# Aligned overflow joins, zero products around the expert stages, a later first map, all next keys in the layer change, and a shared final scaling

## The chip, the cores and the metric

One core of one Trainium2 chip. The time is that of the device in microseconds, from the first to the last work of one launch; less is better. All arithmetic is in float32, with products of two-part (high and low) operands where accuracy needs it.

## The reference

Two transformer blocks of two layers each, on 256 tokens of width 1024, one after the other. Cut to what matters here:

```
for l in range(2):                        # first block
    x = layer_norm(alpha * x + mixer(x), ...)            # gated linear attention and spatial gating
    x = layer_norm(alpha * x + mem_xattn(x, mem), ...)   # k = mem @ wk[l], v = mem @ wv[l]
    x = layer_norm(alpha * x + grouped_moe(x), ...)      # 16 experts, top 2 of one group of 4
for l in range(2):                        # second block
    x = x + gate_m * mixer(rmsnorm(x) * (1 + scale_m) + shift_m)
    x = x + gate_f * grouped_moe_2(rmsnorm(x) * (1 + scale_f) + shift_f)
out = rmsnorm(x, final_norm)
# an expert: y += gate[:, e] * ((silu(x @ w_gate[e]) * (x @ w_up[e])) @ w_down[e])
```

## The kernel before

Everything is one program of straight code on the five engines, with a scheduler that orders the instructions of each engine by priority (the order of the source, and `tc.high_priority` ahead of it) and a simulated time line, except where an order is fixed: inside the expert loop PE runs in the order of the source (`tc.manual_schedule`), and in `start()` PE, DVE and ACT do. `tc.issue_after(ins)` puts what it encloses behind an instruction. Weights come through one DMA queue (SP) into rings of buffers.

There are four expert stages (`moe`): layers 0 and 1 of the first block (stages 1 and 2), layers 0 and 1 of the second (stages 3 and 4). A stage begins with `start()`: the choice of two experts for every token on DVE, five small position products (`pos`), then `gather` products that collect the tokens of experts 0 to 3 into 64 slots each (`xg`), a quarter of the features at a time, with an affine map out of PSUM on ACT or DVE. For features 512 and up the gathers need the second half of the low part `yzl`, written by `low(1)`. The gate weights of the map are written to `turner`. Then, expert by expert:

- `turned` and `down` of the expert before (`ht`, `dn`), `slot_map` (`one` on DVE, `pt` on PE, `pmap` and `wcol` on DVE), the gate and up products of this expert (`front`, tile `gu`, 32 products each), with `down` of the expert before behind the second of the eight steps of the gate product, and for expert 0 `rest()` behind the fourth: the gathers of features 512 and up;
- an overflow test, `tc.If(counts[e] > 64)` (L949): for the rare expert with over 64 tokens a long body follows that works through the rest (`overflows`, with its own tests at L818 and L820). All others jump past it. Each engine has its own copy of the branch. `foretell` puts a hint of the coming branch into PE's code;
- `scatter` of the expert before into four accumulators `y` (L773), and for the next four experts two gathers at a time.

After the last expert `finish_now` scales its result (`ds`) and scatters it (L768). `busy(ins, n)` issues n products of a zero matrix of 128x512 into an accumulator; the kernel before uses it in the overflow bodies alone, and `awake` is a similar helper at the end of stage 2.

Between stage 1 and the next layer ("the layer change") the first half of the memory keys of layer 1 is made (`mem_k(l + 1, kT, 0, memT)`), each weight row split into a high part on ACT (L165) and a low part on DVE (L166); the second half is made in `mem_kv` of layer 1, behind the first mixer. The layer norm between them (`residual_ln`) has priority, and `token_major` (L480, L487, L488) is the row-wise scaling that is put off. `ada` products and sums (L1231, L1236) prepare the modulation of the second block all along.

At the end `rms_tokens` squares y on ACT, a chain of small DVE operations (`rsqrt`, L304 to L313) gives the scale, and four DVE operations (L1789) write z, each followed by its store on SP (L1790).

Of the kernel before, what the change touches and what calls it, by code (L numbers as in the profile page):

```python
# [10 lines left out]
FT = mybir.dt.float32  # L11
# [4 lines left out]
OP = mybir.AluOpType  # L16
# [4 lines left out]
D = 1024  # L21
# [53 lines left out]
def kernel(ctx: ExitStack, tc: tile.TileContext, a: dict, out: bass.AP):  # L75
# [105 lines left out]
    def affine(dst, src, scale, bias, eng=None):  # L181
        e = eng
        if e is None:
            turn[0] += 1
            e = "S" if turn[0] % 2 else "V"
        if e == "S":
            S.activation(dst, src, AF.Identity, bias=bias, scale=scale)  # L187
        else:
            V.tensor_scalar(dst, src, scale, bias, op0=OP.mult, op1=OP.add)
# [444 lines left out]
    def moe(second, lg, rows, rs, nb, c, g, b, names, l, between):  # L634
# [41 lines left out]
        def gather(sel, xg, w, f0, bank):  # L676

            per = 512 // w
            ps = bank("xg", (128, per, w))
            for j in range(per):  # L680
                fs = slice((f0 + j) * 128, (f0 + j + 1) * 128)
                for i, z in enumerate((zh, zh, zl, zl)):
                    PE.matmul(ps[:, j, :], z[:, i % 2, fs], sel[:, i % 2, :], start=i == 0, stop=i == 3)  # L683
            turn[0] += 1
            for j in range(per):
                f = f0 + j
                affine(xg[:, f, :], ps[:, j, :], g[:, f:f + 1], b[:, f:f + 1], "SV"[turn[0] % 2])

        def front(hs, xs, ws, bank, w=64, early=lambda ins: None, half_way=lambda: None):

# [162 lines left out]
        def start():  # L853

            for tt in range(2):
                V.scalar_tensor_tensor(p[:, tt, :], lg[:, tt, :], rs[:, tt:tt + 1], c[:, 0, :], op0=OP.mult, op1=OP.add)
            normal(0, 0)
            if second:
                S.activation(w, p, AF.Exp, scale=-1.0)
            else:  # L860
                mx = tiny("mx", [128, 2])
                V.tensor_reduce(mx, p, axis=AX.X, op=OP.max)
                V.tensor_tensor(w, p, mx[:, :, None].to_broadcast([128, 2, E]), op=OP.subtract)
                S.activation(w, w, AF.Exp)
            high(0, 0)
            for q, tt in ((0, 1), (1, 0), (1, 1)):
                normal(q, tt)
                high(q, tt)
            if second:
                with tc.issue_after(last[1]):  # L870
                    residual(0, 3 - l)
                V.tensor_scalar(w, w, 1.0, None, op0=OP.add)
                V.reciprocal(w, w)
                V.tensor_tensor(p, w, rb[:, 1:2, :].to_broadcast([128, 2, E]), op=OP.add)
                mb = select_top2(p, p)
            else:
                for tt, c_ in ((0, 1), (1, 0), (1, 1), (0, 0)):
                    PE.matmul(y[tt][c_], zerob, zerob[:, None, :].to_broadcast([128, 4, 128]), start=True, stop=False,
                              skip_group_check=True)
                mb = select_top2(p, w)  # L880
            pp = wk("pos", (128, 3, E))
            PE.matmul(pp[:, 0, :], before, mb[:, 0, :], start=True, stop=True)
            PE.matmul(pp[:, 1, :], onesb, mb[:, 0, :], start=True, stop=False)
            PE.matmul(pp[:, 1, :], before, mb[:, 1, :], start=False, stop=True)
            PE.matmul(pp[:, 2, :], onesb, mb[:, 0, :], start=True, stop=False)
            PE.matmul(pp[:, 2, :], onesb, mb[:, 1, :], start=False, stop=True)
            if second:
                residual(3 - l, 4)
            low(0)
            V.scalar_tensor_tensor(posm, pp[:, 0:2, :], 1.0, mb, op0=OP.add, op1=OP.mult)  # L890
            sel = choose(0, 4, posm)
            V.tensor_copy(cnt, pp[0:1, 2, :])
            xg = slots_of(0)
            turn[0] = 0
            gather(sel, xg, 256, 0, wk)
            gate = gates(mb, w)
            rest_ = tiny("grest", [128, 2, E])
            V.tensor_copy(gparts[:, :, :, 0], gate)
            V.tensor_tensor(rest_, gate, gparts[:, :, :, 0], op=OP.subtract)
            V.tensor_copy(gparts[:, :, :, 1], rest_)  # L900
            V.tensor_tensor(gparts[:, :, :, 2], rest_, gparts[:, :, :, 1], op=OP.subtract)
            low(1)
            gather(sel, xg, 256, 2, wk)
            return sel, xg

        for tt in range(2):
# [2 lines left out]
            sel, xg = start()  # L909

        def rest():
            nonlocal gh
            for f0 in (4, 6):
                gather(sel, xg, 256, f0, wk)
            if not second:
                gh = between()
# [6 lines left out]
            with tc.issue_after(ins):  # L923
                tc.mark_branch_hint_location(f"over{second}{l}{e}", engines=[mybir.EngineType.PE])

        gh, late, pend = None, [], None
        more(len(ring) + 1 - FIRST)
        with tc.manual_schedule(engines={mybir.EngineType.PE}):
            for e in range(E):
                i = e % 4  # L930
                ws = weights[e]
                hs, hp = t1("hs", [128, 256]), t1("hp", [128, 2, 128])
                counts[e] = nc.values_load(cnt[0:1, e:e + 1], min_val=0, max_val=T)
                if pend:
                    hs_, hp_, wd = pend
                    turned(hp_, hs_, wk)
                maps_, maps = (maps, mapped(e)) if e else (None, mapped(e))
                xs = xg[:, :, i * 64:(i + 1) * 64]

                def early(ins):  # L940
                    if e < 2:
                        foretell(e, ins)
                    if pend:
                        finish(down(hp_, wd, wk), maps_[1], ds)
                        more(2)

                front(hs, xs, ws, wk, early=early, half_way=(lambda: None) if e else rest)
                more(4 - (e == ONCE // 6))
                with tc.If(counts[e] > 64, label=f"over{second}{l}{e}"):  # L949
                    overflows(e, ws)  # L950
                if pend:
                    ins = scatter(maps_[0], ds)
                    if e + 1 < E:
                        foretell(e + 1, ins)
                if i == 2 and e + 2 < E:
                    nsel = choose(e + 2, 4, posm)
                    nxg = slots_of(e // 4 + 1)
                    for f0 in range(0, NK, 2):
                        late.append(lambda f0=f0, s_=nsel, x_=nxg: gather(s_, x_, 256, f0, wk))
                for _ in range(2):  # L960
                    if late:
                        late.pop(0)()
                if e == 0:
                    if second:
                        gh = between()
                    else:
                        residual()
                pend = hs, hp, ws[2]
                if i == 3 and e + 1 < E:
                    sel, xg = nsel, nxg  # L970
            turned(hp, hs, wk)
            finish_now(down(hp, ws[2], wk), maps[1], maps[0], ds)
        return y


# [158 lines left out]
    def mem_kv(l, kT=None):  # L1134

        memT = memory()
        first = kT is None
        if first:
            kT = keys()
        vm = b8("vm", (128, 2, D))  # L1140
        V.memset(vm[:, 0, 0:1], 0.0)
        if l == 0:
            more = tables()
            next(more)
        if first:
            mem_k(l, kT, 0, memT)
        mem_k(l, kT, 1, memT)
        if l == 0:
            list(more)
        fill("c", l)  # L1150
        for q in range(2):
            for tt, p in enumerate(proj(cut("wv_x", l, cuts=CUT512, i=q), 0, 512, memT, "vmp")):
                cp(vm[:, tt, q * 512:(q + 1) * 512], p)
        return kT, vm
# [585 lines left out]
    for l in range(DEPTH):  # L1740
# [8 lines left out]
                lambda: token_major(rows, rows_of(l, 1, "xtok"), place=rows, wait=True))  # L1749
        if l + 1 < DEPTH:  # L1750
            memT, kT = memory("xl"), keys()
            mem_k(l + 1, kT, 0, memT)
            residual_ln(y, l, 2)
        else:
            rs = last_ln(y, l)
    for l in range(DEPTH):
# [23 lines left out]
        else:  # L1780
            fB = act.tile([128, D], FT, name="fB", tag="b4", bufs=4)
            src = a["final_row"]
            SP.dma_start(fB, bass.AP(tensor=src.tensor, offset=src.offset, ap=[[0, 128], [1, D]]))
    rs = rms_tokens(y)
    for tt in range(2):
        z = act.tile([128, D], FT, name="z", tag="z", bufs=4)
        for q in range(2):
            s = slice(q * 512, (q + 1) * 512)
            V.scalar_tensor_tensor(z[:, s], y[tt][q], rs[:, tt:tt + 1], fB[:, s], op0=OP.mult, op1=OP.mult)  # L1789
            SP.dma_start(out[0, tt * 128:(tt + 1) * 128, s], z[:, s])  # L1790


def _lay(w, cuts):
# [142 lines left out]
```

## Time and profile before

| | |
|---|---|
| median of 3 runs | 1836.7 us (1836.13 to 1842.41) |
| profiled execution | 1834.16 us, span 1832.4 us |
| mean granted clock of TensorE | 0.967 |
| PE busy | 1677.5 us (92%) |
| DVE, ACT busy | 882.6 us, 597.6 us |
| DMA | 570.44 MB, mean 311 GB/s; about 411 GB/s in the expert stages |

PE is TensorE's matrix unit, PEld its weight loads, PEq (or PEldq) its sequencer. "A <- B" in a view of waits says that A on its engine sat idle until B was done; "issue" means that the profile shows nothing that it waited for. Times inside the span are counted from its start. [...]

### The profile page before, as it was taken

How to read it: one execution, taken by the hardware profiler on the slowest of the kernel's cores; microseconds unless marked ns; L12 is line 12 of the kernel's file. 1: busy time of each engine (PE TensorE's matmuls, PEld its weight loads, DVE VectorE, ACT ScalarE, POOL GpSimd, SP SyncE). 2: the span in 40 equal slices, each digit the busy share in tenths (PEclk: the TensorE clock that was granted, in tenths of full speed). 3: DMA queues.
4: the chain of work that ended last, by engine and by line, in shares of the span. 5: the costliest groups of instructions: out<-in, count | busy, mean ns of one | idle time of the engine just before them, and what ended most of it. 6: DMA issues, size and time to landing. Idle time of an engine off the chain costs nothing. (4 is left out here: it accounts for less than half of the span.)

```text
span 1832.4 us, 31259 instructions
## 1 busy us (share of the span) xinstructions
PE 1677.5 (92%) x12127; PEld 1178.6 (64%) x12127; DVE 882.6 (48%) x2328; ACT 597.6 (33%) x1277; POOL 1.6 (0%) x10
## 2 busy tenths in 40 slices
PE   8999989998897998999989998898989899898987
PEld 7799855555686996555548776555545777554553
DVE  7887542222589966222247686322222546432322
ACT  5555322112364554111124554211111444221111
POOL 0000000000000000000000000000000000000000
PEclk9999989999898999999999999999999988999998
DMA  9758779999675786899997455899964872799793
GB/s 371 277 188 343 275 303 391 412 411 403 277 283 182 276 329 225 355 412 411 410 402 308 176 189 199 321 384 413 413 270 154 357 290 99 293 413 412 288 413 126
DMA packets 105790, 570.44 MB, mean 311 GB/s; under 512 B 11725, under 2 KB 14575, under 8 KB 56088
## 3 DMA queue, kind: packets, MB, share of 16 engines
q1 hardware_dynamic: 105064, 566.15, 78.5%
q8 instruction: 181, 2.97, 0.7%
q14 instruction: 113, 0.93, 0.1%
q10 hardware_dynamic: 432, 0.40, 0.1%
HBM read 565.44 MB, written 3.16 MB: 310 GB/s over the span
## 5 line engine op out<-in xcount | busy, mean ns | idle before, releaser
L696 PE MATMUL gu<-w,xg 128*64 128x256 f32 x4096 | 476.1, 384 | 11.9 <-ACT xg L187 8.3
L696 PEld LDWEIGHTS gu<-w,xg 128*64 128x64 f32 x4096 | 297.1, 138 | 184.1 <-issue 40.2
L165 ACT ACTIVATE wp<-w 128x512 fp32r<-128x512 f32 (+5 forms) x416 | 224.8, 548 | 220.7 <-PE pj L494 77.5
L166 DVE TENSOR_TENSOR wp<-w,wp 128x512 fp32r<-128x512 f32 (+5 forms) x416 | 235.8, 584 | 92.0 <-ACT wp L165 90.2
L724 PE MATMUL dn<-w,hp 128*64 128x512 f32 x1024 | 242.0, 609 | 9.5 <-issue 8.1
L724 PEld LDWEIGHTS dn<-w,hp 128*64 128x64 f32 x1024 | 79.4, 141 | 133.8 <-issue 113.8
L494 PE MATMUL pj<-xh,wp 128*128 128x256 f32 x800 | 155.8, 292 | 6.0 <-DVE wp L166 4.8
L494 PEld LDWEIGHTS pj<-xh,wp 128*128 128x128 f32 x800 | 129.3, 196 | 9.7 <-DVE wp L166 5.3
L756 DVE SCALAR_TENSOR_TENSOR ds<-dn,wcol,ds 64x512 fp32r<-64x512 f32 x60 | 45.0, 750 | 179.9 <-ACT ds L755 167.9
L703 DVE TENSOR_TENSOR hs<-hs,gu 128x256 f32<-128x256 f32 x64 | 26.9, 421 | 204.3 <-ACT hs L702 203.2
L494 PE MATMUL pj<-xl,wp 128*128 128x256 f32 x400 | 114.5, 288 | 0.3 <-DVE xl L166 0.3
L702 ACT ACTIVATE hs<-gu 128x256 f32<-128x256 f32 x64 | 24.5, 384 | 231.5 <-PE gu L696 231.0
L755 ACT ACTIVATE ds<-f,onesf 64x512 fp32r<-64x512 f32 x60 | 43.2, 720 | 170.0 <-DVE f L747 169.3
L773 PE MATMUL y<-ds,pmap 128*128 128x512 f32 x240 | 70.8, 417 | 27.6 <-PEq L949 25.5
L755 ACT ACTIVATE ds<-dn,wcol 64x512 fp32r<-64x512 f32 x60 | 40.9, 682 | 169.2 <-PE dn L724 144.8
L747 DVE SCALAR_TENSOR_TENSOR f<-dn,wcol,gh 128x512 f32<-128x512 f32 x32 | 24.0, 751 | 147.2 <-PE dn L724 138.2
L494 PEld LDWEIGHTS pj<-xl,wp 128*128 128x128 f32 x400 | 78.4, 196 | 1.1 <-DVE xl L166 0.5
L773 PEld LDWEIGHTS y<-ds,pmap 128*128 128x128 f32 x240 | 40.9, 190 | 58.4 <-issue 41.3
L1236 DVE SCALAR_TENSOR_TENSOR as<-w,cs,as 128x512 f32<-128x512 f32 x91 | 67.9, 746 | 0.5
L683 PE MATMUL xg<-sel,yzh 128*128 128x256 f32 x256 | 54.0, 291 | 8.9 <-issue 5.1
L756 DVE SCALAR_TENSOR_TENSOR ds<-f,onesf,ds 64x512 fp32r<-64x512 f32 x60 | 44.9, 748 | 22.4 <-ACT ds L755 21.4
L683 PE MATMUL xg<-sel,yzl 128*128 128x256 f32 x256 | 52.6, 288 | 0.0
(546 smaller groups left out, 2493.4 us busy)
## 6 DMA issues: line engine op xcount, KB each, us to landing
w<-in_moe_w_gate_dram SPq DMA_DIRECT2D x54, 1024.0 KB, 10.7
w<-in_ada_w_dram SPq DMA_DIRECT2D x48, 1024.0 KB, 6.9
w<-in_w_down_dram SPq DMA_DIRECT2D x44, 1024.0 KB, 15.0
w<-in_moe_w_up_dram SPq DMA_DIRECT2D x44, 1024.0 KB, 12.6
w<-in_w_up_dram SPq DMA_DIRECT2D x40, 1024.0 KB, 12.0
w<-in_w_gate_dram SPq DMA_DIRECT2D x38, 1024.0 KB, 12.2
w<-in_moe_w_down_dram SPq DMA_DIRECT2D x34, 1024.0 KB, 12.5
w<-in_moe_w_down_dram SPq DMA_DIRECT2D x60, 512.0 KB, 12.6
```

Of the source, the lines that this page charges most:

```text
L165: ins = S.activation(hi, src, AF.Copy)
L166: eng.tensor_tensor(lo, src, hi.bitcast(FT), op=OP.subtract)
L494: ins = PE.matmul(out, lhs[x], rhs[y], start=first and i == 0, stop=last and i == 2, **kw)
L683: PE.matmul(ps[:, j, :], z[:, i % 2, fs], sel[:, i % 2, :], start=i == 0, stop=i == 3)
L696: end = PE.matmul(gu[c * w:(c + 1) * w, i, :], xs[:, k, :], ws[i][k][:, c * n:(c + 1) * n], start=k == 0, stop=k == NK - 1)
L702: S.activation(hs, gu[:, 0, :], AF.Silu)
L703: V.tensor_tensor(hs, hs, gu[:, 1, :], op=OP.mult)
L724: last[2] = PE.matmul(dn[c * w:(c + 1) * w, o:o + n], lhs, wd[2 * k + c * n // 512][:, o:o + n], start=k == 0 and n == 512, stop=k == 3, s ...
L755: S.activation(d[s, c, :], f[s, :], AF.Copy, scale=wc[s, :])
L756: V.scalar_tensor_tensor(d[o, c, :], f[s, :], wc[s, :], d[s, c, :].bitcast(FT), op0=OP.mult, op1=OP.subtract)
L773: ins = PE.matmul(y[tt][c], pt[:, tt, :], d[:, c, :], start=False, stop=False, skip_group_check=True)
L1236: V.scalar_tensor_tensor(s, t[:, i, :], ck, s, op0=OP.mult, op1=OP.add)
```

## The change

- In every overflow body, last: a directive on PE, so that the loader pads the code and the next instruction lies 164 slots past a multiple of 256 instruction slots; where more than 8 slots of padding are needed, the code jumps over them.
- In `start()`: six zero products behind the position products (first block), four behind the second gather (both blocks). `gather` returns its last product for that.
- The first expert's map is no longer made ahead of its gate product, but in `rest()`, ahead of the gathers there.
- Behind the last `down` of a stage: seven zero products.
- Both halves of the next layer's keys are made in the layer change.
- At the end, y times the final gain is formed on DVE while ACT squares y; the scale is then applied by ACT to the first half of the tokens and by DVE to the second, with stores on the queues of ACT and SP.

```
@@ def gather
-                    PE.matmul(ps[:, j, :], z[:, i % 2, fs], sel[:, i % 2, :], start=i == 0, stop=i == 3)
+                    end = PE.matmul(ps[:, j, :], z[:, i % 2, fs], sel[:, i % 2, :], start=i == 0, stop=i == 3)
...
+            return end.ins
@@ def start
-            PE.matmul(pp[:, 2, :], onesb, mb[:, 1, :], start=False, stop=True)
+            ins = PE.matmul(pp[:, 2, :], onesb, mb[:, 1, :], start=False, stop=True).ins
+            if not second:
+                busy(ins, 6)
...
-            gather(sel, xg, 256, 2, wk)
+            busy(gather(sel, xg, 256, 2, wk), 4)
@@ def rest
-            nonlocal gh
+            nonlocal gh, maps
+            maps = mapped(0)
             for f0 in (4, 6):
                 gather(sel, xg, 256, f0, wk)
@@ the expert loop
-                maps_, maps = (maps, mapped(e)) if e else (None, mapped(e))
+                if e:
+                    maps_, maps = maps, mapped(e)
...
                 with tc.If(counts[e] > 64, label=f"over{second}{l}{e}"):
                     overflows(e, ws)
+                    PE.addr_align(256, offset=164, max_nops=8)
...
             turned(hp, hs, wk)
-            finish_now(down(hp, ws[2], wk), maps[1], maps[0], ds)
+            dn = down(hp, ws[2], wk)
+            busy(last[2], 7)
+            finish_now(dn, maps[1], maps[0], ds)
@@ def mem_kv
         if first:
-            mem_k(l, kT, 0, memT)
-        mem_k(l, kT, 1, memT)
+            for q in range(2):
+                mem_k(l, kT, q, memT)
@@ the layer change
             memT, kT = memory("xl"), keys()
-            mem_k(l + 1, kT, 0, memT)
+            for q in range(2):
+                mem_k(l + 1, kT, q, memT)
             residual_ln(y, l, 2)
@@ the end
-    rs = rms_tokens(y)
-    for tt in range(2):
-        z = act.tile([128, D], FT, name="z", tag="z", bufs=4)
-        for q in range(2):
-            s = slice(q * 512, (q + 1) * 512)
-            V.scalar_tensor_tensor(z[:, s], y[tt][q], rs[:, tt:tt + 1], fB[:, s], op0=OP.mult, op1=OP.mult)
-            SP.dma_start(out[0, tt * 128:(tt + 1) * 128, s], z[:, s])
+    ss = tiny("rst", [128, 2, 2])
+    zs = [act.tile([128, D], FT, name="z", tag="z", bufs=4) for _ in range(2)]
+    for q in range(2):
+        s = slice(q * 512, (q + 1) * 512)
+        for tt in range(2):
+            S.activation(t2("sqj", [128, 512]), y[tt][q], AF.Square, accum_out=ss[:, tt, q:q + 1])
+            V.tensor_tensor(zs[tt][:, s], y[tt][q], fB[:, s], op=OP.mult)
+    rs = mean_rs(ss, 2)
+    for q in range(2):
+        s = slice(q * 512, (q + 1) * 512)
+        for tt in range(2):
+            if tt:
+                V.tensor_scalar(zs[tt][:, s], zs[tt][:, s], rs[:, tt:tt + 1], None, op0=OP.mult)
+            else:
+                S.activation(zs[tt][:, s], zs[tt][:, s], AF.Copy, scale=rs[:, tt:tt + 1])
+            (SP if tt else S).dma_start(out[0, tt * 128:(tt + 1) * 128, s], zs[tt][:, s])
```

## Rows read from the trace of the kernel before

**Rows 1.** The page, busy us (share of the span) and instructions.
```profile
PE 1677.5 (92%) x12127; PEld 1178.6 (64%) x12127; DVE 882.6 (48%) x2328; ACT 597.6 (33%) x1277; POOL 1.6 (0%) x10
```
**Rows 2.** Waits of PE: who waited for whom, us in total, times, longest.
```profile
PE y L773 <- PEq L949: 25.5, 52, 2.9
...
PE dn L724 <- issue: 8.1, 4, 3.1
...
PE pt L736 <- DVE turner L901: 7.0, 4, 2.1
...
PE xg L683 <- issue: 5.1, 2, 2.5
...
PE pt L736 <- issue: 3.9, 2, 2.0
...
PE gu L696 <- issue: 2.7, 2, 1.8
PE y L768 <- ACT ds L762: 2.5, 2, 1.7
```
**Rows 3.** PE's branches of L949: ns min/median/max, first and last start; then two single ones.
```profile
L949 PEldq COMPARE_BRANCH  x64: 74/438/5017, 247.6 to 1811.1; - x64
...
L949 PEldq COMPARE_BRANCH  x1: 448/448/448, 262.3 to 262.3; - x1
...
L949 PEldq COMPARE_BRANCH  x1: 2627/2627/2627, 1740.6 to 1740.6; - x1
```
**Rows 4.** Timeline of PE, first and last of the ten straight stalls: start, us, [idle before].
```profile
268.39 0.95 PE L696 MATMUL gu<-w,xg 128*64 128x256 f32 x6 [1.77 <-issue]
...
1748.91 0.24 PE L736 MATMUL pt<-turner,one 128*128 128x176 bf16 x1 [1.87 <-issue]
```
**Rows 5.** Windows: an expert without stall; another from its join, in two parts.
```profile
321.96:334.14 12.18, 12.02 (x92) 6.80 (x90) 2.81 (x7) 2.13 (x4) 0.00 (x0) 1.00 1.02 414
423.71:430.36 6.65, 6.49 (x46) 3.49 (x44) 1.31 (x5) 0.77 (x2) 0.00 (x0) 1.00 1.01 409
430.36:435.55 5.19, 5.19 (x46) 3.04 (x44) 1.50 (x2) 1.36 (x2) 0.00 (x0) 1.00 1.01 416
```
**Rows 6.** Windows: PE, PEld, DVE, ACT, POOL busy, PEclk, DMA share, GB/s.
```profile
269.04:272.45 3.41, 3.41 (x11) 1.85 (x9) 0.00 (x0) 0.00 (x0) 0.00 (x0) 0.50 1.03 423
```
**Rows 7.** Timeline of PE, first gate products of stages 1 and 4.
```profile
238.75 3.40 PE L696 MATMUL gu<-w,xg 128*64 128x256 f32 x16
...
1574.61 1.95 PE L696 MATMUL gu<-w,xg 128*64 128x256 f32 x16
```
**Rows 8.** PE's branches of L818, inside the overflow bodies.
```profile
L818 PEldq COMPARE_BRANCH  x5: 76/196/6465, 1333.4 to 1717.5; - x5
```
**Rows 9.** Timeline of DVE at the start of stage 1.
```profile
237.71 1.29 DVE L846 TENSOR_TENSOR yzl<-z,yzh 128x512 fp32r<-128x512 f32 x2
...
239.32 4.62 DVE L480 TENSOR_TENSOR z<-z,lnrow 128x1024 f32<-128x1024 f32 x4
```
**Rows 10.** Timeline of PE, zero products of `awake` at full clock.
```profile
965.02 2.76 PE L331 MATMUL awake<-zerob 128*128 128x512 bf16 x12
```
**Rows 11.** Windows of the layer change, and of the place of the second half.
```profile
490.40:499.30 8.90, 3.58 (x23) 2.55 (x23) 8.71 (x14) 5.99 (x11) 0.00 (x0) 0.91 0.61 236
497.73:504.56 6.83, 5.26 (x23) 5.26 (x24) 6.83 (x12) 2.04 (x5) 0.00 (x0) 0.50 0.00 0
600.00:620.00 20.00, 20.00 (x171) 19.58 (x170) 19.48 (x46) 10.77 (x20) 0.00 (x0) 1.00 0.83 297
```
**Rows 12.** Timeline of DVE at the end.
```profile
1826.50 2.73 DVE L1789 SCALAR_TENSOR_TENSOR z<-y,rs,fB 128x512 f32<-128x512 f32 x4
```
**Rows 13.** Last gate weights of stage 2: issues, us to landing; their product on PE.
```profile
L145 SPq DMA_DIRECT2D w<-in_w_gate_dram x2: 328/330/333, 915.6 to 916.9; - x2
...
DMA to landing us min/median/max: 16.2/16.2/16.2
...
936.01 1.08 PE L696 MATMUL gu<-w,xg 128*64 128x256 f32 x8
```

More of the change, by code (lines that the diff above doesn't have):

```diff
@@ L924, in foretell @@
                 tc.mark_branch_hint_location(f"over{second}{l}{e}", engines=[mybir.EngineType.PE])
-        gh, late, pend = None, [], None
+        gh, late, pend, maps = None, [], None, None
         more(len(ring) + 1 - FIRST)
```

## The prediction

> **What bounds the kernel now.** I read the page first: PE is busy 1677.5 us of the 1832.4 us span [rows 1], so what can be won is mostly its 155 us of idle time and the stretches in which it runs at half clock. Next I read PE's waits [rows 2]. Two groups have no data behind them: 25.5 us in 52 waits ahead of the first scatter (L773) behind a branch of its own sequencer (L949, the overflow test), and 8.1 + 5.1 + 3.9 + 2.7 = 19.8 us in 10 waits inside straight code with no releaser ("issue"). The reader is to see that these lie in the four expert stages (248 to 482, 735 to 955, 1154 to 1428 and 1582 to 1822 us), where 64 experts follow one another.
>
> The branches themselves [rows 3] last 438 ns in the median, but up to 5017 ns. An undisturbed one leaves PE 0.16 us idle; of the long ones the first 2.15 us or so are hidden by products already queued. The straight stalls [rows 4] come in one place: the first ends at 268.39, 5.7 us after its join (262.25 + 0.448 = 262.70); the last at 1748.91, also 5.7 us after (1740.61 + 2.627 = 1743.24). All ten end 5.6 to 6.0 us after a join, whatever PE did between. So I read both as waits for code: a jump sets off a fetch of what follows, which takes about 5.8 us; where the code in hand ends sooner, PE starves, and where a branch comes too soon after such a border, its target is late. An undisturbed expert takes 12.18 us [rows 5] (14.9 with gathers), and the weights come at 414 GB/s meanwhile with the DMA engines full: DMA is close behind PE.
>
> **Part 1, the joins aligned.** The directive stands at the end of each overflow body. It places the instruction behind it, the join, 164 slots past a multiple of 256. From there to the next multiple are 92 slots, and the next branch follows 90 to 125 slots behind that (180 to 218 PE instructions lie between branches). Without a stall the first 90 take 6.65 us, the rest 5.19 us [rows 5] (from 4.8 to 8.0 us over the experts); with the queue's 2.15 us on top of each, both cover 5.8 us, the second by only about 1 us. So I expect almost every long branch and straight stall to go. Joins: 25.5 - 52 x 0.16 = 17.2 us. Straight code: 19.8 us. [...] Together 44.3 us. The bounds are 0 (the directive does not act) and 44.3 us. Padding costs nothing on the path, since the branch jumps past it; the three executed bodies pay a jump, 0.2 us each by the shorter branches at L818 [rows 8].
>
> [...]
>
> **Part 2, starts of the stages.** PE now waits for the gate weights of the map (turner, 7.0 us in four starts [rows 2]) before the first gate product. With the map behind four of the eight steps of that product, the product starts some 2 us earlier, but the gathers behind it need the second half of yzl, which DVE ends at 239.0 in stage 1 [rows 9]; they ran at 242.08. The limit is then 3 us in stages 1 and 2. There DVE also fills the time with four L480 of 1.2 us ahead of the affine that PE waits for next [rows 9]; if all four stay ahead the gain is nothing. I take the middle, with one or two ahead: 2 us each (0 to 3.3). In stages 3 and 4 yzl is ready 0.7 us before the gathers started: 0.7 and 0.6. A zero product costs 2.76 / 12 = 0.23 us [rows 10], so the six added behind the position products (1.4 us) fit the 1.6 us that PE waits there for sel, and the four behind the gather stand where turner was waited for; if the half-clock stretch that runs there (it makes the first gate products of stage 1 slow [rows 7]) goes with them, that is in the 2 us. Sum 5.3 us.
>
> **Part 3, closing zero products.** Seven take 1.6 us. In stage 4 PE waits 1.67 us there for ds [rows 2], so nothing is lost, and in stage 3 ada products that can move fill that time. In stage 2 the wait is the other 0.85 of these 2.5 us: 0.6 us lost. In stage 1 PE has key products to do and pays all 1.5 us. Cost 2.1 us, bounds 0 and 3.
>
> **Part 4, all keys in the layer change.** The second half's products (12.6 us of PE) leave the stretch from 607 to 620 us, where PE never idles [rows 11], and go behind the first half. There PE works only 3.58 of 8.90 us [rows 11], and runs at half clock from 497.7 to 504.6 [rows 11]. So of the 12.6 us some 5.3 fill idle time and up to 3 come back by the clock; most that can be won is 8 us. But DVE is busy 8.71 of those 8.90 us and 19.48 of 20 us at the old place [rows 11], and eight weight splits of 0.69 us come with the products, 5.5 us. If DVE decides, the layer change grows by more than its old place shrinks: a loss of up to 3 us. Two more 1 MB loads pass the SP queue ahead of the ada loads; DMA moves 236 GB/s there, so they fit. Nearer to the PE bound, because the row-wise scaling on DVE can wait: 5 us won.
>
> **Part 5, the end.** Four final multiplies, 2.73 us in a row on DVE [rows 12], each with its store behind it, become two on each of ACT and DVE behind the scale, while y x fB runs under the squares, and two queues store: the last store starts some 1.2 us earlier (0.5 to 1.6).
>
> **Sum.** 44.3 + 5.3 + 5 + 1.2 - 2.1 = 53.7 us. I keep 2.5 us back for stalls that remain where the margin is 1 us: 51.2. The profiled execution took 1834.16 us (span 1832.4), which gives 1783; the median of the three runs lies 2.5 us higher, so **1785 us**.
>
> **The rivals.** (a) *Straight stalls stay.* The joins are repaired, but issue gaps go on, since code behind a join must still be fetched across a border. For it: one border remains per expert. Against it: the ten stalls end at a fixed time after a join. [...]
> (b) *The weights become the bound.* The last gate weights of stage 2 were issued by 916.9 and landed 16.2 us later, at 933.1; their product began at 936.01 [rows 13]: a lead of 2.9 us, in stage 1 9.5 us. Before that point PE wins about 8.6 and 13.5 us, so 5.7 + 4.0 us would be waited back: 1795. Against it: buffers come free earlier too, and early in stage 2 DMA ran at 357 GB/s, with room to 411; and the second half of the landed weights is needed 5 us later. In stages 3 and 4 leads of 18 us exceed the gain.
> (c) *The directive does not act*, because the slots that count are others than those I count: stalls are only dealt anew, 1785 + 44 = 1829.
> (d) *Slower: every expert gets the bad place.* With one fixed place, a fetch longer than the 92 slots stalls not 30% of the experts but all. One branch at L818 did last 6465 ns [rows 8]. Past 6.65 us each of 60 joins pays the excess; the saving is gone at an excess of 51 / 60 = 0.85 us, a fetch of 7.5 us; at 7.7 us it is 1785 + 60 x 1.05 = 1848. Against it: none of the ten needed over 6.0 us, at full DMA load.
>
> **Numbers.** Chances: forecast 0.62, (a) 0.14, (b) 0.12, (c) 0.07, (d) 0.05. The likeliest case alone spans 1773 (parts 2 to 5 at their best) to 1797 (at their worst). The range for eight in ten reaches over (b) and (a): 1772 to 1812. A measurement tells about 0.5%, 9 us, from no change: faster than 1827.5 are the forecast, (a), (b) and a little of (c), 0.89; within 0.5%, 0.06; slower, 0.05.
>
> **What the next profile would show.** Right: L949 on PE no longer lasts several us, "y L773 <- PEq" near 8 us, no PE wait on issue in the experts, no half clock inside the stages, no wait on turner, PE busy at 490 to 499 us. Wrong: issue gaps 92 slots behind the joins (a, d), PE waits on DMA of w at the last experts of stages 1 and 2 (b), long branches as before (c), or kp later by over 8 us in the layer change behind DVE.

## The result and the profile after

The changed kernel takes 1791.49 us (median of 5 runs, 1788.79 to 1794.61) against 1836.13 us before: ratio 0.9757, 95% interval [0.9736, 0.9777], 44.6 us less. The profiled execution took 1792.45 us (span 1790.6). The prediction was 1785 us, 1772 to 1812, by cleared joins.

The page of the changed kernel, busy us of each engine:

```profile
PE 1671.1 (93%) x12183; PEld 1165.3 (65%) x12183; DVE 882.2 (49%) x2330; ACT 597.9 (33%) x1279; POOL 1.6 (0%) x10
```

PE's idle time (span less busy) falls from 154.9 us [rows 1] to 119.5 us; its busy time falls by 6.4 us although it runs 56 instructions more. These 56 are the zero products: at 0.23 us each [rows 10], some 13 us of the former idle time are only filled by them (an estimate). Its waits, in the columns of [rows 2]; L774 and L954 are the old L773 and L949:

```profile
PE y L774 <- PEq L954: 8.9, 56, 0.2
...
PE ap L1249 <- DVE rsh L311: 6.1, 1, 6.1
...
PE y L774 <- PEq L823: 4.1, 1, 4.1
PE xr L796 <- issue: 3.9, 1, 3.9
...
PE y L769 <- ACT ds L763: 3.4, 1, 3.4
...
PE gu L697 <- DVE xg L189: 2.7, 2, 1.4
...
PE y L653 <- PEq L954: 1.5, 2, 1.4
PE gu L697 <- DMA w<-in_w_gate_dram: 1.5, 1, 1.5
```

Ahead of the first scatter PE now idles 0.16 us, 56 times, the price of an undisturbed branch. The waits on issue in straight expert code and those on turner are gone. What has come in their place stands in five rows: two in an executed overflow body (L796, L823), one on weights (L697 on DMA), one in the layer change (L1249), and one at the starts of stages 1 and 2 (L697 on DVE xg, the affine map of the gathered tokens). The branches, in the columns of [rows 3] (all; then the first of stage 2 and the first of stage 3):

```profile
L954 PEldq COMPARE_BRANCH  x67: 74/359/3522, 243.9 to 1769.1; - x67
...
L954 PEldq COMPARE_BRANCH  x1: 3522/3522/3522, 714.8 to 714.8; - x1
...
L954 PEldq COMPARE_BRANCH  x1: 2554/2554/2554, 1134.8 to 1134.8; - x1
```

Only these two last over 2 us. Ahead of each lies the whole stretch between two stages, in which no join stands.

The windows view of the changed kernel, first to last overflow test of each expert stage and the stretch between the first two (columns as in [rows 6]):

```profile
243.91:450.75 206.84, 198.72 (x1424) 114.73 (x1422) 52.54 (x126) 39.44 (x74) 0.00 (x0) 0.99 1.00 400
450.75:714.82 264.07, 246.91 (x1704) 208.03 (x1702) 206.26 (x489) 132.84 (x258) 0.00 (x0) 0.96 0.74 276
714.82:921.83 207.01, 198.78 (x1423) 115.76 (x1421) 50.14 (x123) 37.44 (x72) 0.30 (x1) 0.99 0.99 398
...
1134.79:1390.14 255.35, 233.38 (x1754) 134.89 (x1752) 71.13 (x164) 43.27 (x82) 0.00 (x0) 0.97 0.86 346
...
1552.19:1769.10 216.91, 209.52 (x1629) 122.08 (x1627) 65.73 (x151) 41.39 (x78) 0.00 (x0) 1.00 0.94 378
```

The same stretches cut at the same tests (start of the branch's record) in all profiles, us:

| kernel | to stage 1 | stage 1 | 1 to 2 | stage 2 | 2 to 3 | stage 3 | 3 to 4 | stage 4 | to the end |
|---|---|---|---|---|---|---|---|---|---|
| before | 247.6 | 221.5 | 266.4 | 208.9 | 210.0 | 262.1 | 165.3 | 229.4 | 21.27 |
| changed | 243.9 | 206.8 | 264.1 | 207.0 | 213.0 | 255.3 | 162.1 | 216.9 | 21.54 |
| changed, again | 243.5 | 206.6 | 263.9 | 207.1 | 212.3 | 255.0 | 162.4 | 216.9 | 21.54 |
| joins only | 246.1 | 205.2 | 274.4 | 205.8 | 217.4 | 254.4 | 160.5 | 216.9 | 21.28 |
| all but joins | 245.4 | 216.3 | 260.9 | 215.8 | 209.9 | 258.1 | 159.0 | 223.3 | 21.53 |
| directive inside | 244.9 | 206.8 | 262.9 | 206.0 | 211.2 | 251.2 | 160.5 | 216.7 | 21.54 |
| keys back | 244.1 | 206.9 | 260.5 | 204.7 | 213.1 | 256.8 | 163.6 | 216.9 | 21.55 |
| no start zeros | 244.7 | 206.8 | 261.7 | 206.0 | 211.5 | 255.4 | 158.5 | 217.5 | 21.55 |
| start as before | 246.6 | 206.9 | 268.0 | 206.0 | 213.3 | 254.5 | 162.8 | 217.5 | 21.54 |
| no closing zeros | 244.2 | 206.8 | 265.8 | 204.2 | 213.2 | 255.6 | 155.7 | 217.4 | 21.28 |
| three edits | 243.7 | 206.5 | 262.1 | 204.2 | 213.3 | 250.9 | 163.8 | 216.7 | 21.10 |
| four edits | 244.8 | 207.1 | 266.4 | 205.5 | 210.9 | 251.3 | 160.6 | 217.3 | 21.09 |

From before to changed the four stages win 14.6 + 1.9 + 6.8 + 12.5 = 35.8 of 41.8 us. The sum of the four goes by the place of the join: 921.9 us before, 913.4 without the directive, 882.3 to 886.1 in the seven profiles with the join at 164 and the directive at the end of the body, 878.3 to 881.1 in the three with it inside. Stages 1 and 4 win fully: from test to test nearly every expert takes 12.2 us, or 14.9 with gathers, where before single ones took up to 18.8. Half clock inside the stages (a granted clock of 0.50), which was to vanish, falls from 30.7 to 20.5 us, 13.7 of them at the expert with two bodies. Stages 2 and 3 give some of it back at single places, which the timeline of PE in the changed kernel shows:

```profile
540.17 0.66 PE L1249 MATMUL ap<-as,onesf 128*32 128x128 f32 x8 [6.14 <-DVE rsh L311]
...
911.91 1.64 PE L697 MATMUL gu<-w,xg 128*64 128x256 f32 x8 [1.46 <-DMA w<-in_w_gate_dram]
...
1339.37 1.22 PE L796 MATMUL xr<-yzl,ovd 128*128 128x512 f32 x2 [3.92 <-issue]
...
1366.43 2.08 PE L774 MATMUL y<-ds,pmap 128*128 128x512 f32 x4 [4.12 <-PEq L823]
```

At 911.91, in the last expert of stage 2, PE waits 1.46 us for the weights of [rows 13], and 3.4 us at a granted clock of 0.50 follow: this expert takes 16.0 instead of 12.8 us. At 1339 and 1366 PE is inside the one expert with two overflow bodies and at its end; this expert takes 50.6 us instead of 42.2 from its test to the next expert's: 8.4 us given back. (The two experts with a single body take 28.8 and 28.7 us before, 29.0 now.)

### The profile page after: what moved, and what is told of

It is laid out like the page before. It is cut to its first block, busy times and chain, and to the rows that moved or that the text cites. A ratio compares the mean times of both kernels' runs of the same rounds, so it can differ in the third digit from the quotient of the medians.

```text
span 1790.6 us, 31386 instructions
## 1 busy us (share of the span) xinstructions
PE 1671.1 (93%) x12183; PEld 1165.3 (65%) x12183; DVE 882.2 (49%) x2330; ACT 597.9 (33%) x1279; POOL 1.6 (0%) x10
## 5 line engine op out<-in xcount | busy, mean ns | idle before, releaser
L697 PE MATMUL gu<-w,xg 128*64 128x256 f32 x4096 | 468.6, 382 | 13.0 <-ACT xg L187 8.1
L697 PEld LDWEIGHTS gu<-w,xg 128*64 128x64 f32 x4096 | 289.2, 137 | 187.2 <-issue 36.3
L725 PE MATMUL dn<-w,hp 128*64 128x512 f32 x1024 | 233.3, 598 | 1.4 <-ACT hp L712 1.4
L725 PEld LDWEIGHTS dn<-w,hp 128*64 128x64 f32 x1024 | 74.3, 139 | 122.6 <-issue 106.2
L703 ACT ACTIVATE hs<-gu 128x256 f32<-128x256 f32 x64 | 24.6, 384 | 233.9 <-PE gu L697 233.4
L774 PE MATMUL y<-ds,pmap 128*128 128x512 f32 x240 | 70.9, 417 | 14.6 <-PEq L954 8.9
L774 PEld LDWEIGHTS y<-ds,pmap 128*128 128x128 f32 x240 | 40.9, 190 | 45.5 <-issue 37.9
## 6 DMA issues: line engine op xcount, KB each, us to landing
w<-in_w_up_dram SPq DMA_DIRECT2D x40, 1024.0 KB, 14.6
w<-in_moe_w_down_dram SPq DMA_DIRECT2D x60, 512.0 KB, 13.3
```

What stands on the lines that cost most here:

```text
L697: end = PE.matmul(gu[c * w:(c + 1) * w, i, :], xs[:, k, :], ws[i][k][:, c * n:(c + 1) * n], start=k == 0, stop=k == NK - 1)
L703: S.activation(hs, gu[:, 0, :], AF.Silu)
L725: last[2] = PE.matmul(dn[c * w:(c + 1) * w, o:o + n], lhs, wd[2 * k + c * n // 512][:, o:o + n], start=k == 0 and n == 512, stop=k == 3, s ...
L774: ins = PE.matmul(y[tt][c], pt[:, tt, :], d[:, c, :], start=False, stop=False, skip_group_check=True)
```

## The experiments

Each run's ratio stands against the kernel before on the same chip. PE's idle time is span less busy time from the page.

**The changed kernel once more.** No edit.

> The changed kernel itself once more, beside the next three on one chip, to see how far its time and the stretches between its expert stages (264.1, 213.0, 162.1 us) repeat. Expected: 1789 to 1795 us; the expert stages within 1.5 us of 206.8, 207.0, 255.3 and 216.9 us. If the stretches between the stages differ by several us from one profile to the next, differences of that size between the other kernels' stretches show nothing.

1790.84 us, ratio 0.9754 [0.9729, 0.9779]. Each stretch repeats within 0.8 us in this second profile. That is shown for this kernel alone, whose ten runs lie within 6 us; four runs of the joins alone range over 16 us (1797.07 to 1813.12), and five without the directive over 14 (1811.88 to 1826.19, the profiled one being the lowest), with the mean granted clock in step. So a difference of several us in a stretch between the stages may belong to the run, and in the row "all but joins" above all.

**The joins alone, and everything but the joins.** The first adds the one line to the kernel before, the second takes it out of the changed kernel:

```diff
                 with tc.If(counts[e] > 64, label=f"over{second}{l}{e}"):
                     overflows(e, ws)
+                    PE.addr_align(256, offset=164, max_nops=8)
```

> The kernel before with nothing but the aligned joins. Theory (the joins carry nearly all of the gain): the stretches between the expert stages won only 3.65 + 2.3 - 2.9 + 3.2 - 0.2 = 6 us in the changed kernel, so this one should be 5 to 7 us above the changed kernel, 1796 to 1799 us, with y<-PEq at the first scatter near 9 us instead of 25.5 and no issue waits of PE in the straight expert code. Rival (zero products and the late map carry a good part, because the clock or the starts are what was slow): over 1810 us, with half-clock stretches of 3.4 us still inside the stages.

> The changed kernel without the directive, all its other parts kept. Theory: the other parts are worth 5 to 7 us, so 1829 to 1832 us, with long branches (over 2 us) and issue waits inside straight expert code back, in other experts than before since the code in between is of another length. Rival (the parts need one another, or the gain is not from the joins): under 1815 us.

Joins alone: 1804.67 us, 0.9818 [0.977, 0.9866]. All but the joins: 1821.54 us, 0.992 [0.9889, 0.9951]. Both theories missed in part: the joins carry about 33 us (0.0182 of 1836), the other parts about 15, not 5 to 7; 0.9818 x 0.992 = 0.974, so by the ratios the two add up. In the waits of the kernel without aligned joins the stalls are back, in other experts:

```profile
PE y L774 <- PEq L954: 21.2, 54, 2.6
...
PE pt L737 <- issue: 6.3, 3, 2.4
...
PE gu L697 <- issue: 4.7, 2, 2.5
...
PE xg L683 <- issue: 4.6, 2, 2.4
...
PE dn L725 <- issue: 2.7, 2, 1.4
```

All nine straight stalls end 5.65 to 5.92 us after a join, as in the kernel before (5.6 to 6.0). Where the other 15 us come from shows in the joins-only kernel: the stretch from stage 1 to 2 takes 274.4 us there, 8 more than before with the same code in it. PE idles 26.5 us of it (17.2 in the changed kernel), 3.1 of them on the first weights of the layer change, which the faster stage reaches too early:

```profile
462.28 0.58 PE L494 MATMUL pj<-memh,wp 128*128 128x256 f32 x1 [3.10 <-ACT wp L165]
```

This reads as if part of what the joins win is waited back there unless the other parts fill the waits; it is argued from these rows, not shown by an edit. The sums of the table say the same: in the four stages the joins alone win 39.6 us (921.9 to 882.3), but all other stretches together take 919.6 instead of 910.5 us; with the other parts they take 904.5. So those parts win their 15 us outside the stages. In the profile without the directive the stages win 8.5 us too (921.9 to 913.4), though no edit lies in them: the stalls are dealt anew there, as rival (c) had it for the whole.

**The joins elsewhere: 28 slots and 186 slots ahead of the border** (taken to be the next multiple of 256 slots; no row of the kernel before shows where it lies). This is the sharpest test of the fetch theory, since nothing but the place changes. The second kernel has offset=70 in the same line.

```diff
-                    PE.addr_align(256, offset=164, max_nops=8)
+                    PE.addr_align(256, offset=228, max_nops=8)
```

> The changed kernel with the joins placed 228 instead of 164 slots past a multiple of 256, so that 28 slots are left to the next one. Theory (a jump sets off a fetch of the code behind the next multiple which takes about 5.8 us, and PE starves where its code runs out sooner): 28 slots take PE some 2 us (92 take 6.65), so PE stalls about 3.8 us in the straight code of every one of some 60 experts, 28 slots behind the join, 1.4 us of half clock with many of them: 230 to 320 us slower than the changed kernel, 2020 to 2110 us, worse than before. Rival (what helps is only that the padding gives all joins one fixed place, or the block border is crossed almost for free and only jumps cost): 1785 to 1810 us, no issue waits in straight code.

> The changed kernel with the joins 70 slots past a multiple of 256: 186 slots to the next one, which 180 to 218 instructions of PE lie from join to branch. Theory: straight code has over 10 us to the border and never stalls, but in the some 28 experts with gathers the branch follows about 0 to 30 slots behind the border, so its target is asked for while the fetch of the next code has only begun, and PE idles 1 to 2 us there ahead of the first scatter: 30 to 60 us slower than the changed kernel, 1820 to 1850 us, with y<-PEq at 35 to 65 us; in the experts without gathers nothing changes. Rival (only the distance from the join to the border counts, the branch may stand anywhere): the time of the changed kernel, 1787 to 1796 us.

28 slots: 1867.55 us, 1.0175 [1.011, 1.0241], slower than before. Its waits, and the first of its stalls in PE's timeline:

```profile
PE gu L697 <- issue: 37.5, 28, 1.8
PE xg L683 <- issue: 33.9, 22, 1.8
```

```profile
262.40 1.16 PE L774 MATMUL y<-ds,pmap 128*128 128x512 f32 x4 [0.16 <-PEq L954]
...
266.32 0.99 PE L697 MATMUL gu<-w,xg 128*64 128x256 f32 x5 [1.82 <-issue]
```

50 stalls, 71.4 us. All stand 11 or 12 products into the code behind the join; with a weight load for each these are 22 to 24 instructions that the profile shows, just short of the 28 slots up to the border. All but two, behind executed bodies, end 5.0 to 6.4 us after the join (260.29 for the one shown), of which the 15 to 17 products queued ahead of it cover the first part. The rival falls; the mechanism stands, and the stalls come at the place that was taken for the border. The size I expected, 3.8 us each, was wrong: it left out the 2.15 us of queued products that the prediction had counted. 5.8 - 2.0 - 2.15 = 1.65; measured 1.43 on average. Nor did half clock come "with many": it follows three of the stalls in stage 1 and one in stage 4, and the mean granted clock is 0.980.

186 slots: 1836.01 us, 0.9996 [0.9968, 1.0024], within the 1820 to 1850 expected.

```profile
PE y L774 <- PEq L954: 45.4, 54, 2.9
...
PE y L774 <- PEq L821: 7.6, 2, 3.9
```

No wait on issue is left in straight code, and PE idles at branches instead: mostly 1.2 to 1.8 us ahead of the scatter that follows an expert with gathers (the intervals there take about 13.3 or 16.2 us instead of 12.2 or 14.9; most others are unchanged, but for the second of each stage, 2.8 to 5.5 us longer, and those of the executed bodies). By the count of slots these waiting branches stand just behind the border; where the branch stands ahead of it, most intervals are unchanged. So the gain is not that all joins have one place, but which place: with 186 slots the whole change is worth nothing. The four stages together take 965.5 us at 28 slots and 936.4 at 186, against 886.1 at 92.

**The directive inside the innermost body**, which no expert executes here:

```diff
                         overflow(e, 192, 64, *args)
+                        PE.addr_align(256, offset=164, max_nops=8)
...
                     overflows(e, ws)
-                    PE.addr_align(256, offset=164, max_nops=8)
```

> The changed kernel with the directive moved into the innermost nested body (the third 64 tokens of an expert), which no expert here executes, so that the executed overflow bodies run into no padding and the join stands at the same place. Theory (PE pays the padding at the end of the three executed bodies: 4.1 + 0.7 + 0.7 us in the changed kernel): these waits shrink to about 0.2 each, 4 to 5 us faster than the changed kernel, about 1787 us. Rival (the executed bodies cost what they do because of the code fetches behind a border inside them, wherever the padding stands): the same time as the changed kernel within 1 us, the long waits only move.

1782.21 us, 0.969 [0.9661, 0.9718]: the fastest. Stage 3 takes 251.2 instead of 255.3 us. The end of the second body now costs 0.44 us. At its start PE idles 10.0 us in one piece (in the changed kernel 4.9 for DVE's ovd and then the 3.92 on issue), as PE's timeline shows:

```profile
1336.60 1.19 PE L796 MATMUL xr<-yzh,ovd 128*128 128x512 f32 x2 [10.02 <-issue]
...
1360.85 1.19 PE L774 MATMUL y<-ds,pmap 128*128 128x512 f32 x4 [0.44 <-PEq L823]
```

So moving the directive takes some 4 us off stage 3, and a wait inside the bodies remains; both theories are right in part. That the 4 us are the price of the padding is not shown, though: with no directive at all (the kernel without aligned joins) PE waits 3.46 us at the same place, where the kernel before waits 0.43:

```profile
1382.45 1.41 PE L774 MATMUL y<-ds,pmap 128*128 128x512 f32 x4 [3.46 <-PEq L823]
```

So this wait comes with or without padding; that it goes by where the body's code lies is likely, but no edit separates it. The other 5 us are spread over four stretches (1 to 2 us each); one of them is the first branch of stage 2, where the wait of 1.4 us ahead of L653 shrank to 0.2. The rest I can't assign.

**The keys back at the old place.**

```diff
-            for q in range(2):
-                mem_k(l + 1, kT, q, memT)
+            mem_k(l + 1, kT, 0, memT)
```

(and the second half again at its old call in the second layer).

> The changed kernel with the second half of the memory keys back at its old place in the second layer. The prediction put moving it at 5 us won, so by it this kernel takes 1796 to 1797 us and the layer change shows PE idle at half clock again. Rival (VectorE decides there: eight weight splits come with the products, and the stretch from stage 1 to stage 2 shrank by only 2.3 us in the changed kernel, with the start of stage 2 in it): 1789 to 1793 us, no difference that can be told.

1788.40 us, 0.972 [0.969, 0.975]: the move won no 5 us; with 0.9757 [0.9736, 0.9777] for the changed kernel it lost some or nothing. The waits say why:

```profile
PE kp L494 <- DVE xl L166: 3.1, 1, 3.1
...
PE ap L1249 <- DVE rsh L310: 2.2, 1, 2.2
```

The 3.1 us in the layer change (3.4 in the kernel before, part of the idle time in the first window of [rows 11]) are indeed filled by the moved products, but PE then runs ahead of DVE and waits 6.1 us for the same engine at L1249 (540.17 above), where without the move it waits 2.2 us, and 2.3 at L1094. From stage 1 to 2 PE idles 15.8 us without the move and 17.2 with it. The DVE rival holds.

**Starts as before, and all stores on SP**; two edits far apart.

```diff
-                if e:
-                    maps_, maps = maps, mapped(e)
+                maps_, maps = (maps, mapped(e)) if e else (None, mapped(e))
...
-            busy(gather(sel, xg, 256, 2, wk), 4)
+            gather(sel, xg, 256, 2, wk)
...
-            (SP if tt else S).dma_start(out[...], zs[tt][:, s])
+            SP.dma_start(out[...], zs[tt][:, s])
```

> Two edits far apart, each read by its own stretch of the profile. First: the starts of the stages as before (no zero products there, first map ahead of the gate products). The changed kernel reached the first overflow test of stage 1 3.65 us earlier than before. Theory (the late map and the zero products win that): the stretch up to that branch grows from 243.9 to about 247.5 us, the start of stage 2 by 1 to 2 us, with the waits on turner back. Rival (most of the 3.65 us came from elsewhere ahead of the stage): under 245 us. Second: all four final stores on SP's queue instead of two on SP's and two on ACT's. Theory (the stores from ACT land 3.2 us after their issue and those from SP 2.0): from the last branch to the end 20.5 us instead of 21.5. Rival (the end is set by when rs is ready): 21.4 to 21.9 us.

1798.79 us, 0.9807 [0.9757, 0.9858]. The first test of stage 1 comes at 246.6, 2.7 us later than in the changed kernel; 7.3 us of waits on turner are back. The end is 21.54 us as before the edit: my theory of ACT's late stores falls.

**Without the start's zero products**, the map still late:

```diff
-            if not second:
-                busy(ins, 6)
...
-            busy(gather(sel, xg, 256, 2, wk), 4)
+            gather(sel, xg, 256, 2, wk)
```

> The changed kernel without the six and four zero products at the starts; the first map stays behind half of the first gate products. With both edits undone the first overflow test of stage 1 came 2.7 us later (246.6 instead of 243.9). Theory of the prediction (the zero products cost and bring nothing by themselves, the moved map wins): 243.5 to 244.3 us up to that branch. Rival (the zero products keep the clock up at the start, where without them the first products ran at half clock for 3.4 us): 245 to 246 us, with a half-clock stretch before 244 us. In all within 3 us of the changed kernel.

1789.28 us, 0.9748 [0.9722, 0.9774], the time of the changed kernel. The first test comes at 244.7: of the 2.7 us the map wins about 1.9, the zero products about 0.8 (without them half clock runs for 3.4 us from 233.4).

**Without closing zero products, end as before.**

```diff
             dn = down(hp, ws[2], wk)
-            busy(last[2], 7)
             finish_now(dn, maps[1], maps[0], ds)
```

(and the old final loop of four multiplies and stores on SP.)

> Two edits far apart, each read by its own stretch. First: the changed kernel without the seven closing zero products at the end of each expert stage. By the prediction they cost 1.5 us in stage 1 and 0.6 us in stage 2, so the stretches from stage 1 to 2 and 2 to 3 shrink by about that (264.1 to 262.6, 213.0 to 212.4). Rival (they keep the clock: before, half clock ran from 456.8 for 6.8 us at the end of stage 1, with them only for 3.4): the stretches stay or grow by up to 2 us and the half-clock stretch of 6.8 us at the end of stage 1 is back. Second: the end as before (four final multiplies on DVE behind the scale, all stores on SP). Theory (the shared scaling gains nothing since the fourth multiply by the final row delays the scale by 0.6 us and ACT's stores land late): 21.3 us from the last branch to the end instead of 21.5. Rival (the prediction's 1.2 us): 22.7 us.

1787.24 us, 0.9751 [0.9699, 0.9804]. The stretches 1 to 2 and 2 to 3 don't shrink (+1.8, +0.2), 3 to 4 does, by 6.4. The end takes 21.28 us, less than the shared scaling's 21.54.

**Three edits together, then four**: directive inside, keys back, only three multiplies by the final row ahead of the scale; the fourth leaves out the closing zero products too.

```diff
-            V.tensor_tensor(zs[tt][:, s], y[tt][q], fB[:, s], op=OP.mult)
+            if q * tt == 0:
+                V.tensor_tensor(zs[tt][:, s], y[tt][q], fB[:, s], op=OP.mult)
...
+            if q * tt:
+                V.scalar_tensor_tensor(zs[tt][:, s], y[tt][q], rs[:, tt:tt + 1], fB[:, s], op0=OP.mult, op1=OP.mult)
-            if tt:
+            elif tt:
```

> Changed kernel with three edits: the directive inside the innermost overflow body (in the earlier run 9 us faster than the changed kernel, 4 of them in stage 3), the second half of the keys back at its old place (3 us faster), and only three of the four multiplies by the final row ahead of the scale, the fourth fused with it. Theory for the last (the whole end hangs on the first store: it is over 5.1 us after that store is issued, in all forms tried, and the fourth multiply holds the scale up by 0.6 us): 20.9 to 21.1 us from the last branch to the end instead of 21.5; in all 1775 to 1781 us. Rival (the gain of the moved directive beyond 4 us, and that of the keys, were the luck of the clock between the stages): 1784 to 1789 us.

> The kernel of the run before (directive inside, keys back, three multiplies) without the closing zero products too. By the prediction these cost 2.1 us, so 2 us faster, 1773 to 1779 us. Rival (in the earlier run without them the stretches from stage 1 to 2 and from 2 to 3 did not shrink, and the 6 us between stages 3 and 4 were the clock's): the same time as the run before within 2 us.

Three: 1782.88 us, 0.970 [0.9673, 0.9728]. Four: 1787.09 us, 0.9734 [0.9707, 0.976]. Three edits beat both kernels, but are no faster than the directive inside alone (0.969): putting the keys back brings nothing that adds to it. The end is 21.10 us, as the theory said. Leaving out the closing zero products cost 4 us here (stretch 1 to 2 grew by 4.3), after winning up to 4 by the medians on the other base, where the ratios (0.9757 and 0.9751) tell no difference.

## Why the prediction was right, point by point

**The mechanism holds.** A jump is followed by a wait, read as one for code, whose end comes about 5.8 us after the join (5.0 to 6.4 over the straight stalls of three kernels), and how much code stands ahead of the next border decides whether PE starves there or at the next branch. Both sides were moved at will, to 50 straight stalls and to 45.4 us at the branches. The prediction took the border to be the next multiple of 256 slots, which no row of the kernel before shows. The runs fit it: with 28 slots the stalls stand 22 to 24 listed instructions behind the join, and with 92 and 186 no wait on issue is left in straight expert code; no other spacing was tried. Crossing it in straight code soon after a jump cost 71.4 us in 50 crossings in the 28-slot kernel. Rival (a) falls, since no wait on issue is left in straight expert code with 92 slots, and rival (c) with the rows of L954. Rival (d) was a real danger, by the place and not by a longer fetch: at 28 slots the kernel is 1.75% slower. Its price was too high, since it let every excess over 6.65 us cost and left out the queued 2.15 us that Part 1 counts.

**The terms.**

| term | predicted | measured |
|---|---|---|
| joins, straight stalls, half clock | 44.3 | 35.8 in the four stages, with two losses in it: 8.4 in the double-body expert, 3.2 at the end of stage 2; 47.4 without them; alone, 33 in all |
| starts | 5.3 | 2.7 in stage 1 (2 predicted); 7 in all by the medians with and without, 9 by the ratios, not resolved by stage |
| closing zero products | -2.1 | not resolved: by the medians, leaving them out made one kernel 4 us faster, another 4 us slower |
| keys in the layer change | +5 | 0 or a loss of up to some 3 us |
| end | +1.2 | -0.27 |
| these four together | 9.4 | 15, in the kernel without aligned joins; also 15 outside the stages, changed against joins alone (one profile each) |
| kept back | -2.5 | the losses of 8.4 + 3.2 |

The 44.3 us are 17.2 at the joins, 19.8 in straight code and 7.3 for half clock behind five stalls. No run shows this last term by itself; the granted clock shows half clock in the stages falling from 30.7 to 20.5 us, and in [rows 7] 16 gate products take 1.45 us longer in stage 1 than in stage 4.

That the total came within 6.5 us of the forecast is in part luck: misses of both signs met. Step by step:
- *Starts*: in stage 1 the middle that was taken came true as reasoned: two of the four L480 stand ahead of the affine (237.94, 2.35 us on DVE, in the changed kernel), and PE waits 1.4 us for it at 240.80.
- *Bodies, "0.2 us each"*: mis-sized. The expert with two bodies lost 8.4 us: PE waits 3.92 us at the start of its second body, which it didn't before, and 4.12 at the end instead of 0.43. Moving the directive inside brought 4 us back, but without any directive, all other parts kept, the expert takes 45.8 us, no less than the 46.3 with it inside, and waits 3.46 at the end. So some 4 us of the loss aren't the directive's, and neither wait is shown to be the padding's. That both come from where the body's code now lies is argued, not shown.
- *Rival (b), the weights*: it came true at one of its two places, at a third of its size. The last expert of stage 2 waits 1.46 us for gate weights and runs 3.4 us at half clock; stage 1 has no such wait.
- *Keys*: the failed step is "nearer to the PE bound, because the row-wise scaling on DVE can wait". The place named was right (the 3.4 us went), but PE then waits 6.1 us behind the same engine at L1249; that next wait was not looked for.
- *End*: the step that failed is "the last store starts some 1.2 us earlier". It did start 0.85 us earlier after the last test (before 1829.25, now 1786.38), but that sets nothing: in five kernels (before, changed, stores on SP, end as before, three edits) the end comes 5.10 to 5.13 us after the first store is issued.

The timeline of the changed kernel at the end (DVE, ACT, and the queues that issue the stores):

```profile
1782.65 0.68 DVE L1799 TENSOR_TENSOR z<-y,fB 128x512 f32<-128x512 f32 x1
1783.25 0.16 DVE L304 TENSOR_SCALAR rsm<-rsm 128x2 f32<-128x2 f32 x1
...
1785.02 1.34 ACT L1807 ACTIVATE z<-z,rs 128x512 f32<-128x512 f32 x2 [2.54 <-DVE rs L313]
1785.02 0.88 DVE L1805 TENSOR_SCALAR z<-z,rs 128x512 f32<-128x512 f32 x2
1785.54 0.82 SPq L1808 DMA_DIRECT2D out_dram<-z  x2
1785.77 0.96 ACTq L1808 DMA_DIRECT2D out_dram<-z  x2
```

The first store is issued at 1785.54, the span ends at 1790.64, 5.1 us later; before, 1827.28 and 1832.38, also 5.1. The sharing halves what follows the scale, and the four stores of 256 KB then move back to back, in one stretch of some 2.7 us in both kernels. The first store itself came later, since the fourth multiply (1782.65) stands between the squares and L304. With that one fused behind the scale, the end came 0.44 us earlier.

**What stays open.** The stretches between the stages differ by up to 10 us between kernels whose code there is the same or nearly so, and one profile of a kernel need not stand for all its runs; PE's idle time and the granted clock change with them (mean clock 0.967 before, 0.976 changed, 0.970 with the joins alone). Which edit sets which of these stretches was not separated, so the 15 us of the parts beside the joins are shown as a sum only. That faster stages lengthen the stretches behind them is suggested by the joins alone and by the kernels with 28 and 186 slots, whose slow stages go with 898.6 and 898.0 us outside them (904.5 in the changed kernel, with the same code); the cause is open.

## What to carry to other kernels

Where a kernel jumps over rarely used code, look in the waits for a releaser that is only the engine's own sequencer or nothing at all, and measure their distance from the last jump: if it is constant (here 5.0 to 6.4 us), the place of the join among the instructions may be a knob: moving it from 92 to 28 slots ahead of the border cost 4.3% here (ratios 1.0175 and 0.9757). Of the two bodies that took the padding, the one that isn't executed gave the faster kernel (0.969); measure the executed bodies again afterwards, since their own waits may change: here one went from 0.43 to 4.12 us. A wait that is filled with moved work is won only if the engine that caused it doesn't hold up the next step (here 3.4 us were filled, and 6.1 us waited for the same engine at L1249): follow that engine, not the wait.

## What the runs showed that was not expected

- In the second overflow body, executed once, PE waits 3.92 us on issue right behind a wait of 4.9 us for data: read as a wait for code, this rare body pays for that as well as for its work. Neither the kernel before nor the one without the directive has this wait; that it too goes by place is argued, not shown.
- A stall of 1.4 us on average in 50 experts left the clock nearly untouched (mean granted clock 0.980, 4 half-clock stretches behind 50 stalls), where four of the ten straight stalls of the kernel before, of up to 3.1 us, were followed by one (a fifth stretch followed a long branch).
- Two profiles of one kernel agreed within 0.8 us in each of nine stretches, but runs of the same program on the same chip differed by up to 16 us in other kernels. Edits that touch none of a stretch's code go with differences of several us in it (1 to 2: 274.4 with the joins alone, 266.4 before).
